# A hybrid stack on one core: the order on TensorE set by another estimate of the engines

## The chip, the cores and the metric

The kernel runs on one core of a Trainium2 chip. The metric is the device time of one execution in microseconds; the time of a kernel is the median of its runs. PE is TensorE, DVE is VectorE, ACT is ScalarE, POOL is GpSimd, SP is SyncE.

## The reference

`reference(...)` takes 256 tokens of width 1024 in fp32 through two blocks. The first block has two layers. Each norms x, multiplies by one wide matrix, and feeds the columns to three branches whose outputs are put side by side, multiplied by `w_out` and added to x; a gated product with a per-layer input follows. The second block adds a layer of compressed, selected and windowed attention ("nsa"), a layer of attention with forgetting, both with attention to a memory of 256 further tokens, and a gated convolutional FFN behind each. In short:

```
for l in range(2):                              # first block
    z = rms_norm(x) @ w_in[l]
    y = concat(rwkv7_branch(z_a), dsa_branch(z_b), dilated_branch(z_c))
    x = x + y @ w_out[l];  x = x + gated(rms_norm(x), p[l])
x = rms_norm(x)                                 # second block
x = x + nsa_mixer(...) @ w_o[0];    x = x + conv_ffn(...)
x = x + forgetting(...) @ w_o[1];   x = x + conv_ffn(...);   out = rms_norm(x)
```

The recurrent branch `rwkv7_branch` is a scan over tokens with a 64x64 state for each of 6 heads.

## The kernel before

All of it is one function, `tile_hybrid_stack`. Weights stream from DRAM in blocks of 128 rows. The products are to be exact to fp32: ACT rounds a block to its high part `whi`, DVE or GpSimd subtracts it from the raw block for the low part `wlo` (rows `wlo<-wraw,whi`), the activations are split likewise (`k` and `k`), and each product is made in three passes, high by high, high by low, low by high. So a dense product in the trace is a group of three rows on `pz`, each of 128x256 or so, and a block of weights of 128x512 costs ACT and one of DVE and GpSimd an operation.

Work is written as generators ("streams") that emit a step at a time. `Flow.run` runs the streams of a stage together and decides which emits next. There are nine stages: mixer of layer 0, its gate, mixer of layer 1, its gate, nsa mixer, FFN, forget mixer, FFN, last norm. In a stage run for instance the dense products (`dense`), the recurrent chain (`rwkv_chain`, with gram products, the turning of k by transposes into `bkt`, levels, chunks and a group norm), the sparse and dilated attention, the norm's factors (`stats`, `norm_norm_stats`) and the loading of weights (`loading`).

Only PE's order is fixed by the emission (`tc.manual_schedule(engines={PE})`). Which stream emits next follows from an estimate of time: `Flow.tensor` reckons each PE instruction, `Flow.note` each one of the other engines with a rate per element (table `RATE`), and `Clock.settle` lets every engine that is free start the first instruction that is ready, as if the engines did not touch each other. The orders on DVE, ACT, GpSimd and SP are made by the compiler's scheduler from the emitted program, and so change with it. Each engine runs its own queue strictly in order.

Names in what follows: in the first block's mixers the head sums are products of a constant with `k` into a tile of 128x2 (L616, in `rwkv_chain`, for `bon`). In the nsa mixer `norm_norm_stats` makes 1/sqrt by three Newton steps on GpSimd (tiles `rs_t` and `rs_y` of 128x1, two of each for each half of the tokens), DVE writes a diagonal matrix from the result (`diag`), and PE multiplies it by ones (`po<-diag,ones`) so that the factors lie along the columns in all rows. `cmp_part` makes the compressed keys' and values' inputs, `cmp_keys`, `cmp_values` and `cmp_attend` go on from there, `mem_prep` prepares the memory. L616 is the product, L621 the transpose and L458 the place from which all other engines' instructions are issued, so rows are told apart by tiles. `out_rows` sets up the loads of `w_o` in the second block and names the events that they wait for; its first group of layer 0 waits for none.

Of the kernel before, what the change touches and what calls it, by code (L numbers as in the profile page):

```python
# [110 lines left out]
class Ev:  # L111
    """A point in the emission that other streams can wait for."""
# [9 lines left out]
class Fork:  # L122
    """A stream to be started that the one that yields it doesn't wait for."""
# [6 lines left out]
# For each run of streams: the time to allow for what may come in between, and that from or to the tensor engine.  # L130
# [6 lines left out]
class At:  # L137
    """The time when some instructions are through, as far as it can be told."""
# [10 lines left out]
class Op:  # L149
    __slots__ = ("lane", "cost", "deps", "start", "end", "ready")  # L150

    def __init__(self, lane, cost, deps, end=math.inf):
        self.lane, self.cost, self.deps, self.end = lane, cost, deps, end


class Clock:
    """Estimates when the engines are through with what has been emitted.

    An instruction's time follows from its size, its dependences from the regions that it reads and writes. An engine
    that is free starts the first of the instructions that are ready. What lies more than PAST before the present  # L160
    is settled for good.
    """

    PAST = 4.0

    def __init__(self):
        self.now, self.dirty, self.pending = 0.0, False, []
        self.free = {name: 0.0 for name in RATE}
        self.free["SP"] = 0.55
        self.used, self.last, self.owner, self.slots = {}, {}, {}, {}  # L170
        self.pool, self.names, self.prior = {}, {}, {}
        self.reach = 0.2
# [11 lines left out]
    def follows(self, pool, old):  # L184
        """Tiles of a pool take the place of those of an earlier one."""
# [17 lines left out]
    def before(self, reads, writes=(), lane=None):  # L203
        """The instructions that one with these operands comes after; engines that read a bank of PSUM take turns."""
# [35 lines left out]
    def put(self, lane, cost, reads, writes, issuer=None):  # L240
# [5 lines left out]
        op = Op(lane, cost, deps)  # L246
# [5 lines left out]
    def settle(self):  # L252
# [3 lines left out]
        free = dict(self.free)  # L256
# [20 lines left out]
        while True:  # L277
            best = None
            for lane, ops in ready.items():
                f = free[lane]  # L280
                for j, (i, op) in enumerate(ops):
                    key = (max(f, op.ready), i)
# [7 lines left out]
            free[lane] = op.end  # L290
            order.append(op)
# [5 lines left out]
        for op in order:  # L297
            if op.start < self.now - self.PAST:
                self.free[op.lane] = op.end
                op.deps = ()  # L300
# [14 lines left out]
class Flow:  # L315
    """Orders the emission of several streams of work by an estimate of the tensor engine's time.
# [2215 lines left out]
```

## Time and profile before

| | |
|---|---|
| runs, median (all) | 1208.56 us (1205.94, 1208.56, 1211.92) |
| profiled execution, span | 1214.1 us |
| PE busy | 1123.1 us, 92% |
| DVE, ACT, POOL busy | 928.3, 727.0, 362.7 us |
| DMA | 168.60 MB, 139 GB/s mean |

The profile is of one execution. It gives busy time for each engine, the clock that PE was granted (1.0 is 2.4 GHz, 0.5 is 1.2 GHz), the chain of work that ended last, and for each wait of an engine what released it. Times of rows are microseconds from the start of the span.

### The profile page before, as it was taken

How to read it: one execution, taken by the hardware profiler on the slowest of the kernel's cores; microseconds unless marked ns; L12 is line 12 of the kernel's file. 1: busy time of each engine (PE TensorE's matmuls, PEld its weight loads, DVE VectorE, ACT ScalarE, POOL GpSimd, SP SyncE). 2: the span in 40 equal slices, each digit the busy share in tenths (PEclk: the TensorE clock that was granted, in tenths of full speed). 3: DMA queues.
4: the chain of work that ended last, by engine and by line, in shares of the span. 5: the costliest groups of instructions: out<-in, count | busy, mean ns of one | idle time of the engine just before them, and what ended most of it. 6: DMA issues, size and time to landing. Idle time of an engine off the chain costs nothing.

```text
span 1214.1 us, 23478 instructions
## 1 busy us (share of the span) xinstructions
PE 1123.1 (92%) x8505; PEld 1000.8 (82%) x8505; DVE 928.3 (76%) x2246; ACT 727.0 (60%) x1642; POOL 362.7 (30%) x355
## 2 busy tenths in 40 slices
PE   6899999988989989979989899999989998999996
PEld 6888887888888867978856899999878867999995
DVE  4889887768898877868777677777777666877786
ACT  4526656656266666666556566666666555766664
POOL 4442213433521226160001612222251124222221
PEclk9879989989899999988979999999989999999999
DMA  7444324444452146647312456666534424666662
GB/s 213 111 125 122 80 53 139 139 140 109 119 141 80 45 134 213 194 116 212 101 35 51 153 152 204 192 187 181 185 92 140 139 84 145 183 191 186 188 183 95
DMA packets 154124, 168.60 MB, mean 139 GB/s; under 512 B 15692, under 2 KB 141532, under 8 KB 154008
## 3 DMA queue, kind: packets, MB, share of 16 engines
q1 hardware_dynamic: 153336, 166.10, 46.9%
q0 software_dynamic: 672, 1.00, 0.4%
q8 instruction: 67, 1.10, 0.4%
q14 instruction: 49, 0.40, 0.1%
HBM read 164.65 MB, written 2.42 MB: 138 GB/s over the span
## 4 chain that ended last, share of the span: by engine, by line
PE 64%; issue 13%; DVE 10%; POOL 8%; ACT 4%; DMA 1%; SPq 0%; ACTq 0%; POOLq 0%; DVEq 0%
PE pz L616 34%; PE po L616 9%; PE pr L616 7%; PE sc L616 7%; POOL k L458 4%; PE tp L616 3%; PE tp L621 3%; POOL wlo L458 2%; DVE k L458 2%; DVE wlo L458 2%; ACT whi L458 2%; POOL rs_t L458 1%; POOL rs_y L458 1%; PE pr L621 1%; DVE zs L458 1%
## 5 line engine op out<-in xcount | busy, mean ns | idle before, releaser
L458 ACT ACTIVATE whi<-wraw 128x512 fp32r<-128x512 f32 (+2 forms) x604 | 371.2, 624 | 248.9 <-PE pz L616 72.5
L458 DVE TENSOR_TENSOR wlo<-wraw,whi 128x512 fp32r<-128x512 f32 (+1 forms) x505 | 365.1, 736 | 141.8 <-ACT whi L458 131.7
L616 PE MATMUL pz<-k,whi 128*128 128x256 f32 x1568 | 314.0, 297 | 7.7 <-ACT k L458 4.9
L616 PEld LDWEIGHTS pz<-k,whi 128*128 128x128 f32 x1568 | 255.8, 200 | 18.5 <-issue 5.8
L458 POOL TENSOR_TENSOR wlo<-wraw,whi 128x512 fp32r<-128x512 f32 (+3 forms) x99 | 132.9, 1344 | 415.9 <-ACT whi L458 378.4
L616 PE MATMUL pz<-whi,k 128*128 128x256 f32 (+5 forms) x1152 | 248.9, 302 | 8.4 <-DVE k L458 5.0
L616 PE MATMUL pz<-k,wlo 128*128 128x256 f32 x784 | 229.1, 292 | 10.2 <-POOL wlo L458 10.2
L616 PEld LDWEIGHTS pz<-whi,k 128*128 128x128 f32 (+1 forms) x1152 | 187.2, 188 | 20.3 <-DVE k L458 6.9
L458 POOL TENSOR_TENSOR k<-yv,k 128x256 fp32r<-128x256 f32 x54 | 95.6, 1785 | 280.8 <-ACT k L458 280.8
L616 PE MATMUL pz<-wlo,k 128*128 128x256 f32 (+5 forms) x576 | 170.6, 296 | 0.1
L616 PEld LDWEIGHTS pz<-k,wlo 128*128 128x128 f32 x784 | 157.2, 200 | 11.5 <-POOL wlo L458 11.5
L616 PE MATMUL po<-k,whi 128*128 128x256 f32 x704 | 132.1, 281 | 0.0
L616 PEld LDWEIGHTS pz<-wlo,k 128*128 128x128 f32 (+1 forms) x576 | 108.5, 188 | 3.3 <-DVE wlo L458 0.6
L616 PEld LDWEIGHTS po<-k,whi 128*128 128x128 f32 x704 | 109.0, 191 | 0.0
L616 PE MATMUL po<-k,wlo 128*128 128x256 f32 x352 | 98.8, 281 | 0.0
L616 PE MATMUL sc<-whi,k 128*128 128x512 f32 x240 | 82.2, 402 | 3.8 <-POOL k L458 3.5
L458 DVE SCALAR_TENSOR_TENSOR k<-zs,convp,k 128x254 f32<-128x254 f32 (+1 forms) x176 | 73.7, 482 | 0.0
L458 ACT ACTIVATE sm<-sm,mn 128x128 f32<-128x128 f32 x100 | 44.4, 445 | 37.9 <-DVE mn L458 37.8
L616 PEld LDWEIGHTS po<-k,wlo 128*128 128x128 f32 x352 | 67.0, 190 | 0.0
L616 PE MATMUL tp<-whi,k 128*128 128x512 f32 x176 | 58.8, 395 | 0.0
L616 PEld LDWEIGHTS sc<-whi,k 128*128 128x128 f32 x240 | 45.1, 189 | 15.9 <-POOL k L458 4.8
L616 PE MATMUL sc<-wlo,k 128*128 128x512 f32 x120 | 47.4, 395 | 0.0
(372 smaller groups left out, 1858.5 us busy)
## 6 DMA issues: line engine op xcount, KB each, us to landing
wraw<-in_w_up_dram SPq DMA_DIRECT2D x88, 512.0 KB
wraw<-in_w_in_dram SPq DMA_DIRECT2D x44, 512.0 KB
wraw<-in_w_down_dram SPq DMA_DIRECT2D x44, 512.0 KB
wraw<-in_w_in_dram SPq DMA_DIRECT2D x32, 256.0 KB
wraw<-in_w_out_dram SPq DMA_DIRECT2D x16, 512.0 KB
wraw<-in_ple_w_gate_dram SPq DMA_DIRECT2D x16, 512.0 KB
wraw<-in_w_o_dram SPq DMA_DIRECT2D x10, 512.0 KB
wraw<-in_w_kv_shared_dram SPq DMA_DIRECT2D x10, 512.0 KB
```

The costliest lines, as they stand in the source:

```text
L458: ins = call(*args, **kw)
L616: nc.tensor.matmul(out_, st, mv, start=start, stop=stop)
L621: nc.tensor.transpose(out_, x, idn)
```

## The change

The estimate of `Flow` and `Clock` is changed in three ways, and one load is held back.

1. Instructions that hold the SBUF port that DVE and GpSimd share are reckoned one after another: every instruction on GpSimd, and on DVE those with more than two elements a row that read more than one larger SBUF operand, or that are a `tensor_scalar` or `tensor_copy` from SBUF to SBUF.
2. `Flow.tensor` reckons 2200 columns a us for fast products of 256 columns or more (2400 before; half of it at the lower clock), and products overlap if they use different row groups or different column groups of the array (16 parts; before 4, by columns alone).
3. The first `w_o` group of the nsa layer is loaded only when all loads of the layer's input weights have begun (`Begun`).

```diff
-        self.quiet, self.issue, self.lanes, self.work = False, 0.0, [0.0] * 4, {}
+        self.quiet, self.issue, self.lanes, self.work = False, 0.0, [0.0] * 16, {}
...
-                    key = (max(f, op.ready), i)
+                    key = (max(f, op.ready, held) if op.port else max(f, op.ready), i)
...
             free[lane] = op.end
+            if op.port:
+                held = op.end
...
-        op = self.clock.put(lane, cost, reads, writes, issuer)
+        port = lane == "POOL"
+        if lane == "DVE" and n > 2:
+            big = [x for x in reads if x.space != PSUM and math.prod(x.shape[1:]) > 1]
+            port = len(big) > 1 or name in ("tensor_scalar", "tensor_copy") and len(big) == 1 and writes[0].space != PSUM
+        op = self.clock.put(lane, cost, reads, writes, issuer, port)
...
-        lanes = range(*(x // 32 for x in (self.clock.region(out)[1], self.clock.region(out)[2] + 31)))
+        r0, r1, c0, c1 = (x // 32 for ap in (st, out) for x in (self.clock.region(ap)[1], self.clock.region(ap)[2] + 31))
+        lanes = [4 * r + c for r in range(r0, r1) for c in range(c0, c1)]
...
+        full = 2200 if mv.dtype != F32 and cycles >= 256 else 2400
...
-            rate = 2400 if self.work.get(k - 1, 0) >= BUSY else 1200
+            rate = full if self.work.get(k - 1, 0) >= BUSY else full / 2
...
+class Begun:
+    def __init__(self, chain):
+        self.chain = chain
+    @property
+    def n(self):
+        return self.chain().left
...
-        u = Load(OP_SHARE, [yT2_ev[l][k] for k in ks] if l or ks != OUT_2[0][0] else ())
+        u = Load(OP_SHARE, [yT2_ev[l][k] for k in ks] if l or ks != OUT_2[0][0] else [Begun(lambda: chains["nsa", 0])])
```

`Chain` counts in `left` the loads that have not begun. No instruction of the program is added or removed on any engine (PE 7649, DVE 2216, ACT 1472, POOL 360, SP 404); about 1090 of PE's change places, 403 in the mixer of layer 0, 424 in that of layer 1, 190 in the nsa mixer, 56 in the forget mixer and under 15 in each other stage. Lines L616, L621 and L458 become L638, L643 and L469.

The first place is on PE in the mixer of layer 0. `pr` with 128x2 are the head sums, `sc` scores of the sparse attention, `pz` dense products with weights `whi` and `wlo`. Before:

```order
L616 MATMUL pz_1148<-whi_0_0_1050,k_1_92 128x256
L616 MATMUL pz_1148<-wlo_0_0_1051,k_1_92 128x256
L616 MATMUL pz_1148<-whi_0_0_1050,k_2_93 128x256
L616 MATMUL pr_1202<-cst_74,k_107_887 128x2 x6
L616 MATMUL sc_1212<-k_6_99,k_132_1114 128x256 x2
L616 MATMUL pz_1148<-whi_2_0_1054,k_1_92 128x256
```

On PE in the same mixer after the change:

```order
L638 MATMUL pz_1368<-whi_4_0_1314,k_3_94 128x256
L638 MATMUL pz_1368<-wlo_4_0_1315,k_3_94 128x256
L638 MATMUL pz_1368<-whi_4_0_1314,k_4_95 128x256
L638 MATMUL pr_1440<-cst_74,k_112_910 128x2 x6
L638 MATMUL pz_1368<-whi_6_0_1324,k_3_94 128x256
L638 MATMUL pz_1368<-wlo_6_0_1325,k_3_94 128x256
```

The head sums stood in the eleventh group of dense products and now stand near the end of the thirteenth; all of the twelfth has moved ahead of them. The mixer of layer 1 shows the same.

The second place is on PE at the start of the nsa mixer. `po<-diag,ones` spreads the norm's factors, `pz<-k,whi` and `pz<-k,wlo` are the products of `cmp_part`, `pz<-whi,mT` those of the memory's values. Before:

```order
L616 MATMUL pz_6955<-k_973_6671,whi_4_0_6947 128x256
L616 MATMUL pz_6955<-k_974_6672,whi_4_0_6947 128x256
L616 MATMUL pz_6955<-k_973_6671,wlo_4_0_6948 128x256
L616 MATMUL po_7032<-diag_6869,ones 128x128
L616 MATMUL po_7032<-diag_6871,ones 128x128
L616 MATMUL pz_6955<-k_973_6671,whi_6_0_6951 128x256
L616 MATMUL pz_6955<-k_974_6672,whi_6_0_6951 128x256
```

On PE at the start of the nsa mixer after the change:

```order
L638 MATMUL pz_6884<-wlo_6_0_6867,mT_6113 128x256
L638 MATMUL pz_6884<-whi_6_0_6866,mT_6114 128x256
L638 MATMUL po_6942<-diag_6852,ones 128x128
L638 MATMUL po_6942<-diag_6854,ones 128x128
L638 MATMUL pz_6884<-whi_6_0_6866,mT_6113 128x256
L638 MATMUL pz_6884<-wlo_6_0_6867,mT_6113 128x256
L638 MATMUL pz_6884<-whi_6_0_6866,mT_6114 128x256
L638 MATMUL pz_6960<-k_971_6669,whi_0_0_6901 128x256
```

The two products have moved from the last sixth of the compression's 48 products to the place ahead of all of them.

The third place is on GpSimd at the same time: its four splits of the compression's weights and the Newton steps. Before:

```order
L458 TENSOR_SCALAR rs_t_6745<-rs_y_6744,ss_6741 128x1
L458 TENSOR_SCALAR rs_t_6754<-rs_y_6753,ss_6739 128x1
L458 TENSOR_SCALAR rs_y_6744<-rs_t_6745,rs_y_6744 128x1
L458 TENSOR_TENSOR wlo_0_0_6902<-wraw_6897,whi_0_0_6901 128x512
L458 TENSOR_SCALAR rs_y_6753<-rs_t_6754,rs_y_6753 128x1
L458 TENSOR_TENSOR wlo_2_0_6906<-wraw_6897,whi_2_0_6905 128x512
```

On GpSimd there after the change:

```order
L469 TENSOR_TENSOR wlo_0_0_6902<-wraw_6897,whi_0_0_6901 128x512
L469 TENSOR_TENSOR wlo_2_0_6906<-wraw_6897,whi_2_0_6905 128x512
L469 TENSOR_SCALAR rs_t_6745<-rs_y_6744,ss_6741 128x1
L469 TENSOR_SCALAR rs_t_6754<-rs_y_6753,ss_6739 128x1
L469 TENSOR_TENSOR wlo_4_0_6953<-wraw_6899,whi_4_0_6952 128x512
L469 TENSOR_SCALAR rs_y_6744<-rs_t_6745,rs_y_6744 128x1
```

Two splits now come ahead of the first Newton step; the second pair of splits lies between the first steps, as before it did a little later.

## Rows read from the trace of the kernel before

**Rows 1.** The page, part 4: the chain that ended last.

```profile
PE 64%; issue 13%; DVE 10%; POOL 8%; ACT 4%; DMA 1%; SPq 0%; ACTq 0%; POOLq 0%; DVEq 0%
```

**Rows 2.** Busy time by stage: window, us, engines' busy (instructions), PEclk, DMA share, GB/s.

```profile
0.00:226.70 226.70, 201.99 (x1662) 177.63 (x1663) 173.60 (x461) 121.21 (x295) 79.75 (x81) 0.94 0.43 117
...
262.00:471.00 209.00, 191.69 (x1644) 168.73 (x1645) 168.17 (x454) 114.67 (x283) 72.03 (x70) 0.94 0.40 111
...
508.00:677.50 169.50, 154.00 (x1061) 125.67 (x1062) 129.25 (x413) 107.87 (x293) 32.98 (x48) 0.91 0.39 110
```

**Rows 3.** Waits of PE by cause: us in total, times, longest.

```profile
PE pz L616 <- POOL wlo L458: 10.2, 6, 3.5
```

**Rows 4.** Timeline of DVE and POOL, 521 to 527 us: start, us, instruction.

```profile
521.96 0.69 DVE L458 TENSOR_TENSOR wlo<-wraw,whi 128x512 fp32r<-128x512 f32 x1 [0.93 <-ACT whi L458]
523.21 2.99 DVE L458 TENSOR_TENSOR wlo<-wraw,whi 128x512 fp32r<-128x512 f32 x1 [0.55 <-ACT whi L458]
...
523.15 2.49 POOL L458 TENSOR_TENSOR wlo<-wraw,whi 128x512 fp32r<-128x512 f32 x2
```

**Rows 5.** Stretches at half clock, columns as in rows 2.

```profile
321.30:328.10 6.80, 6.80 (x30) 6.13 (x30) 6.17 (x10) 1.39 (x2) 3.61 (x2) 0.50 0.29 43
...
532.90:539.70 6.80, 5.02 (x23) 5.02 (x24) 2.13 (x3) 4.44 (x11) 2.70 (x8) 0.50 0.28 76
...
614.80:628.50 13.70, 12.11 (x52) 7.09 (x52) 8.30 (x40) 8.86 (x33) 0.00 (x0) 0.50 0.09 24
```

**Rows 6.** Timeline of PE in both first-block mixers, idle before and releaser in brackets.

```profile
103.71 1.40 PE L616 MATMUL pr<-cst,k 128*128 128x2 f32 x12
...
110.41 0.58 PE L621 MATMUL pr<-cst,bk 64*128 64x64 f32 x6 [1.39 <-ACT bkt L458]
...
176.44 0.63 PE L621 MATMUL tp<-cst,qr 128*128 128x128 f32 x4 [2.22 <-ACT sm L458]
...
201.11 0.49 PE L616 MATMUL pr<-wlo,k 128*128 128x512 f32 x1 [1.30 <-DVE wlo L458]
...
319.41 0.79 PE L616 MATMUL pr<-k,bk 64*128 64x128 f32 x5 [2.19 <-DVE k L458]
...
357.63 0.58 PE L621 MATMUL pr<-cst,bk 64*128 64x64 f32 x6 [1.96 <-ACT bkt L458]
...
426.14 0.63 PE L621 MATMUL tp<-cst,qr 128*128 128x128 f32 x4 [1.22 <-DVE qr L458]
```

**Rows 7.** Timeline of PE at the start of the nsa mixer.

```profile
521.26 0.40 PE L616 MATMUL pz<-k,whi 128*128 128x256 f32 x2
...
524.46 0.39 PE L616 MATMUL pz<-k,wlo 128*128 128x256 f32 x1 [1.36 <-POOL wlo L458]
...
526.16 0.28 PE L616 MATMUL pz<-k,wlo 128*128 128x256 f32 x1
...
528.64 0.29 PE L616 MATMUL pz<-k,wlo 128*128 128x256 f32 x1
...
534.68 0.80 PE L616 MATMUL po<-diag,ones 128*128 128x128 f32 x2 [5.53 <-DVE diag L458]
...
536.56 0.41 PE L616 MATMUL pz<-whi,k 128*128 128x256 f32 x1
```

**Rows 8.** Timeline of POOL there: Newton steps, two in a row.

```profile
526.61 0.66 POOL L458 TENSOR_SCALAR rs_t<-rs_y,ss 128x1 f32<-128x1 f32 x2
...
528.33 1.72 POOL L458 TENSOR_SCALAR rs_t<-rs_y,ss 128x1 f32<-128x1 f32 x2
...
533.53 0.55 POOL L458 TENSOR_SCALAR rs_y<-rs_t,rs_y 128x1 f32<-128x1 f32 x2
```

**Rows 9.** Timeline of PE in the middle and at the end of the nsa mixer.

```profile
562.36 0.28 PE L616 MATMUL pz<-whi,k 128*30 128x256 f32 x1
...
570.44 0.41 PE L621 MATMUL pz<-cst,k 30*128 30x30 f32 x2 [1.88 <-DVE k L458]
...
606.84 1.06 PE L616 MATMUL pz<-kcT,k 128*128 128x32 f32 x8
...
616.35 2.03 PE L621 MATMUL tp<-cst,k 128*128 128x128 f32 x7 [3.62 <-DVE ls L458]
```

More of the change, by code (lines that the diff above doesn't have):

```diff
@@ L149, with __init__ @@
 class Op:
-    __slots__ = ("lane", "cost", "deps", "start", "end", "ready")
-    def __init__(self, lane, cost, deps, end=math.inf):
-        self.lane, self.cost, self.deps, self.end = lane, cost, deps, end
+    __slots__ = ("lane", "cost", "deps", "start", "end", "ready", "port")
+    def __init__(self, lane, cost, deps, end=math.inf, port=False):
+        self.lane, self.cost, self.deps, self.end, self.port = lane, cost, deps, end, port
 class Clock:
@@ L169, in __init__ @@
         self.free["SP"] = 0.55
+        self.port = 0.0
         self.used, self.last, self.owner, self.slots = {}, {}, {}, {}
@@ L238, in when, with put @@
         return max((o.end + self.gap(o.lane, lane) for o in ops), default=0.0)
-    def put(self, lane, cost, reads, writes, issuer=None):
+    def put(self, lane, cost, reads, writes, issuer=None, port=False):
         deps = self.before(reads, writes, lane)
@@ L245, in put @@
             deps = [first]
-        op = Op(lane, cost, deps)
+        op = Op(lane, cost, deps, port=port)
         self.mark(op, reads, writes)
@@ L255, in settle @@
         self.dirty = False
-        free = dict(self.free)
+        free, held = dict(self.free), self.port
         wait = {}
@@ L299, in settle @@
                 self.free[op.lane] = op.end
+                if op.port:
+                    self.port = op.end
                 op.deps = ()
@@ L756, in __init__ @@
         def __init__(self, loads):
-            self.loads, self.ahead, self.then, self.last = iter(loads), None, None, None
+            loads = list(loads)
+            self.loads, self.ahead, self.then, self.last, self.left = iter(loads), None, None, None, len(loads)
         def begin(self):
@@ L762, in begin @@
                 if self.ahead is not None:
+                    self.left -= 1
                     self.ahead.prev, self.last = self.last, self.ahead
```

## The prediction

> **What bounds the kernel now.** I read the page first: the chain that ended last runs over PE for 64% of the span and over waits for other engines for most of the rest [rows 1]. So the time is PE's work plus the places where PE stands still, plus what PE loses by running at the lower of its two clock levels. The table by stage says where that is: PE is idle 24.7 us of the first layer's mixer (226.7 − 202.0), 17.3 us of the second layer's (209.0 − 191.7) and 15.5 us of the mixer that opens the second block (169.5 − 154.0); these three stages also have the low mean clocks, 0.94, 0.94 and 0.91 [rows 2]. Everywhere else PE is nearly full. The order of instructions hardly moves outside these three stages, so the whole answer must come from some 57 us of idle time and the stretches at half clock inside them.
>
> The list of PE's waits names POOL's splitting of weights as the costliest single cause (10.2 us in 6 waits) [rows 3]. One row shows why: VectorE's split of a 128x512 block took 0.69 us while GpSimd was quiet and 2.99 us when GpSimd ran two such splits (2.49 us) over the same stretch [rows 4]. VectorE and GpSimd thus hold up each other, and the planner of before knows nothing of it. The planner's rate for dense products is off too: from the row at 526.16 to that at 528.64, at full clock, PE starts 21 products of 256 columns in 2.48 us, 0.118 us each, some 2170 columns a us where the planner reckons 2400 [rows 7]. The new figures are nearer the trace. That does not settle the time, since the planner only chooses the order on PE, and the orders of the other engines then shift with it.
>
> **The change part by part.** No instruction is added or removed; PE has the same work. The terms are waits that go, waits that come, and clock.
>
> *First layer's mixer.* The head sums of the recurrent branch (the row with 128x2 outputs at 103.71) move behind all of one group of dense products and most of the next. 48 products and some 60 of the next pass them, about 110 × 0.118 = 13 us. The chain that follows (turning k, the levels, the group norm) starts some 13 us later and is left with less other work under it at the end, and the gating work of the other branches comes earlier. Four waits stood behind the old place. The one for the turned k was 1.39 us [rows 6]; ACT's copies stood there behind the scalings of a projection and one weight split, and now directly follow, so I take 0.4 (−1.0). The one for a scaled tile before the transposes at 176.44 was 2.22 us [rows 6]; the gates it waits for now come more than 10 us earlier in all queues: −2.2. The one for w_out's low half at 201.11 was 1.30 [rows 6]; VectorE has less queued there: −1.0. Against it, attention transposes that had cover now lie 3 to 5 us behind what they read. By the nearest rows such a wait costs 0.4 to 2.2 us, and I count two, +2.0. Sum −2.2, ends −4.2 (no new wait) and +0.2 (both at the top).
>
> *Second layer's mixer.* The same move of the head sums, with the same shape of order. The wait for the turned k, 1.96 us, becomes 0.6 (−1.4); the one at 426.14, 1.22, goes (−1.2) [rows 6]; the split of w_out repeats that of the first layer (the row at 201.11 stands for both): −1.0; two new waits of one us less in all than above: +1.5. Here 9 dense products also move ahead of the gram products at 319.41, which waited 2.19 us for VectorE [rows 6]. 9 × 0.118 = 1.0 us of cover: −1.0. The 6.80 us after that wait ran at half clock [rows 5]. If PE stays full through it, 3.4 us come back; I count half, −1.7. Sum −4.8, ends −8 and 0.
>
> *Clock in the two level phases.* The dense work that now runs ahead of the head sums used to fill the stretch of small products behind them. By the orders some 33 dense products lay between the small ones there before, and 12 now. The trace shows no case of that very mix. The nearest row is the tail of the nsa mixer, small products only, where the clock stood at 0.50 for 13.70 us; the other end is no loss, since the first layer's phase ran at full clock before. A stretch of 3.4 us at half clock in one and 0 to 3.4 in the other costs 1.7 to 3.4: I take +2, ends 0 and +7 (13.7 / 2) [rows 5].
>
> *Entry of the nsa mixer.* Here the change costs. The two products that spread the norm's factors over all rows (out of `diag`) stood behind the compression's products and PE reached them late; it still waited 5.53 us for the second one, after 1.36 us for GpSimd's split at 524.46 [rows 7]. They now stand ahead of the compression's 48 products. PE gets there at 521.26 − 3 × 0.118 = 520.9 and stops until the Newton steps on GpSimd are through. How early can that be? The chain's steps are small: two of one kind took 0.66 and two of the other 0.55 when undisturbed, but a pair took 1.72 beside VectorE [rows 8]. The last twelve ran from 528.33 to 534.08, 5.75 us, and undisturbed would take 3 × (0.66 + 0.55) = 3.6. The new orders put VectorE's `diag` writes directly behind one split, so VectorE will mostly wait too and not disturb; I take the spread at 531.5 instead of 534.68, with 534.7 (nothing gained) and 530.6 as ends. From there PE has 2 + 3 + 48 products and, later, the 8 transposes (0.8 us) to catch up. After a stop of 5.53 us the next 6.80 us ran at 0.50 [rows 5, 7], with 0.21 us a product. So 0.4 + 32 products in 6.8 us + 19 × 0.118 = 2.2, and 0.8: PE is even at 541.7. Before it was there at 536.56 with 3.1 us of half clock still ahead, which cost 1.6: 538.1 [rows 5, 7]. Loss 541.7 − 538.1 = +3.6; ends 0 and +7. Behind the waiting spread stand ACT's scalings of x and the splits of the next weights; they have 10 us of idle ahead of PE's need, so nothing more is charged.
>
> After a stop about twice as long the same 6.80 us at half clock are assumed. The Trainium skill, in "TensorE: Matmul & The Clock Gate", section "HAM oscillation", has the same view: each wait that is long enough makes the burst behind it start cold, once, and its price is half of the throttled time. By that the longer stop would cost no more clock than the shorter, as the sum has it; the stretch from 532.90 at 0.50 agrees.
>
> *Middle of the nsa mixer.* The wait for the compressed keys, 1.88 us, stays. From the last of the keys' products (562.36) to their transposes (570.44) lie 8.0 us of work on other engines [rows 9]. For the compressed values PE has 2.9 us of work in that interval where it had 10.3: by the keys' latency a wait of up to 5 us, by the steps' earlier places in VectorE's queue none. I take half, +2.5, ends 0 and +5.
>
> *End of the nsa mixer.* Attention scores and memory transposes move behind the dense products, so that 6.6 us of PE work instead of 4.3 stand between the compressed scores (ending at 607.9) and the transposes that waited until 616.35, 8.5 us later. That wait, 3.62 us and 0.5 more before it, falls to 8.5 − 6.6 = 1.9 [rows 9]: −2.2. Half clock over 13.7 us behind it [rows 5] may shorten a little: −0.3 in the sum, up to −3.5 at the end. Sum −2.5, ends −6 and +1.
>
> The later w_o load has the same place in SyncE's queue, and the forget mixer has a few swaps of neighbours without a long wait beside them: 0, with ±1. PLE gates and both FFNs keep their order: 0.
>
> Sum: −2.2 − 4.8 + 2.0 + 3.6 + 2.5 − 2.5 = −1.4 us. On the profiled execution's 1214.1 that is 1212.7; the profiled execution lies 5.5 us over the median of 1208.56, so 1207.2 in the measure of the runs.
>
> **The rivals.**
>
> *Dense work spent too early (slower).* Place: entry and middle of the nsa mixer and the two level phases. The planner believes PE finds enough between; if the spread is ready only at 534.7, the values wait the full 5 us and one level phase falls to half clock for as long as the tail did, the terms are +7, +5 and +7, against gains of −1, −3 and −2.5: +12.5, some 1221. It decides from about 533.5 on for the spread, with a wait over 3 us at the values. For it: PE does stand for 10 us with 48 products ready behind the spread [rows 7]. Against: GpSimd's queue has nothing else then [rows 8].
>
> *Waits go as planned and the clock stays up (faster).* Gram, tail and level phases keep the full level, no new waits: −4.2 − 8 + 0 + 0 + 0 − 6 = −18; half of that already passes 0.5%. About −12 is its middle: 1196. For it: the costliest cause of PE's waits comes from the contention that the planner now counts [rows 3, 4]. Against: a stall at the nsa entry is in the order itself.
>
> *The change doesn't do what it says.* The planner could still be off by as much as before, since the true durations of GpSimd vary from 0.28 to over 1 us a step [rows 8]: the waits change places and the sum is 0 ± 3, 1208. This lies within the forecast's own band.
>
> **How the numbers follow.** About 0.5%, 6 us, can be told from no change. Forecast (with the third rival inside it): 1207, within 6 us of the median, 0.42. Faster: 0.33. Slower: 0.25. The likeliest case's own range is 1202.5 to 1214.6. The range for 8 in 10 goes to the faster case's middle less some, 1193, and to the slower one's, 1220.
>
> **What would show it.** In the changed profile: PE's wait for `diag` at the nsa entry near 10 us instead of 5.5, and GpSimd's 24 steps closer together; idle before the turned k under 1 us in both layers; no wait at the scaled transposes; w_out's wait under 0.5 us; a wait of 1 to 5 us at the compressed values; idle time at the end of the nsa mixer down to 2 us. Mean clocks: first layer 0.93 to 0.95, second 0.94 to 0.96, nsa 0.89 to 0.92. The forecast is wrong if the level phases lose the clock for long, if the spread comes at 528 or at 536, or if stages whose order hardly moves change by over 2 us.

## The result and the profile after

The changed kernel takes 1269.3 us (median of its runs, 1261.8 to 1269.4) against 1209.2 us of the kernel before on the same chip: a ratio of 1.047, 95% interval 1.044 to 1.050. It is **slower by 4.7%**, and far above the forecast of 1207 and its range of 1193 to 1220. The profiled execution has a span of 1267.6 us, 53.5 more than that of before (1214.1).

The chain that ended last, from the page of the changed kernel (it answers to [rows 1]):

```profile
PE 36%; issue 10%; POOL 5%; DVE 4%; ACT 2%; DMA 1%; SPq 0%; POOLq 0%; ACTq 0%; DVEq 0%
```

This line says little here: only 58% of the span is accounted for, so its falling share of PE is not a finding. The table by stage does better. These are the same three stages of the changed kernel as in [rows 2], with the same columns:

```profile
0.00:241.40 241.40, 207.72 (x1661) 183.47 (x1662) 172.77 (x461) 122.28 (x295) 77.18 (x82) 0.92 0.40 110
276.70:506.60 229.90, 199.91 (x1644) 175.20 (x1645) 171.42 (x454) 114.91 (x283) 73.56 (x70) 0.90 0.36 101
544.20:730.40 186.20, 158.06 (x1061) 127.06 (x1062) 125.78 (x413) 108.48 (x293) 29.23 (x48) 0.88 0.35 100
```

The three stages are 14.7, 20.9 and 16.7 us longer, 52.3 together: practically all of it. The window minus PE's busy time is 33.7, 30.0 and 28.1 us where it was 24.7, 17.3 and 15.5, so PE stands still for 34.3 us more. The other 18.0 us are busy time of PE: the same products take longer. The granted clock fell from 0.94, 0.94 and 0.91 to 0.92, 0.90 and 0.88. With two levels, 1.2 and 2.4 GHz, twice the missing part is the share of time at the lower one: some 38.6, 46.0 and 44.7 us against 27.2, 25.1 and 30.5, by clocks of two digits. PE loses half of such time where it has work, which is at most 23 us in the three and fits the 18.0, since PE also idles at the lower level.

The list of PE's waits by cause, of the changed kernel (us in total, times, longest), has a new head; [rows 3] showed GpSimd's splits there:

```profile
PE po L638 <- DVE diag L469: 11.9, 3, 6.7
PE pr L638 <- DVE s L469: 11.8, 2, 7.3
PE tp L643 <- ACT k L469: 10.7, 3, 5.3
...
PE tp L643 <- DVE kd L469: 5.4, 1, 5.4
...
PE pz L638 <- POOL wlo L469: 3.9, 5, 1.7
```

The wait that the change was aimed at did fall, from 10.2 us to 3.9. The four other rows come to 39.8 us; of these causes the first had 9.1 us before, the second 0.9. The timeline of PE in the two first-block mixers, which answers to [rows 6]:

```profile
88.80 0.61 PE L638 MATMUL pz<-whi,k 128*128 128x296 f32 x1 [2.96 <-DVE zs L469]
...
119.66 0.90 PE L643 MATMUL tp<-cst,qr 128*128 128x128 f32 x3 [3.59 <-ACT k L469]
...
126.31 1.40 PE L638 MATMUL pr<-cst,k 128*128 128x2 f32 x12
...
138.60 1.67 PE L638 MATMUL pr<-k,k 64*64 64x64 f32 x26 [2.59 <-DMA k<-bounce_t]
...
160.07 0.91 PE L638 MATMUL pr<-s,k 64*64 64x64 f32 x12 [4.53 <-DVE s L469]
...
378.29 0.90 PE L643 MATMUL tp<-cst,qr 128*128 128x128 f32 x3 [5.25 <-ACT k L469]
384.12 1.39 PE L638 MATMUL pr<-cst,k 128*128 128x2 f32 x12
...
417.70 0.91 PE L638 MATMUL pr<-s,k 64*64 64x64 f32 x12 [7.29 <-DVE s L469]
```

The head sums (outputs of 128x2) stand at 126.31 in the first layer, where before they stood at 103.71. In both kernels the tile that they read is there at about 88 us. They wait for more, because their stream waits for all that it has emitted, and that includes the small triangular solve on VectorE. Its first and last step in the changed kernel, from VectorE's timeline:

```profile
92.15 0.17 DVE L469 TENSOR_TENSOR r<-r,r 96x15 f32<-96x15 f32 x1
...
108.21 1.27 DVE L469 TENSOR_TENSOR r<-r,r 96x15 f32<-96x15 f32 x1
```

That is 17.3 us. The same steps of the kernel before, from VectorE's timeline:

```profile
92.76 0.39 DVE L458 TENSOR_TENSOR r<-r,r 96x15 f32<-96x15 f32 x2
...
106.69 0.17 DVE L458 TENSOR_TENSOR r<-r,r 96x15 f32<-96x15 f32 x1
```

They took 14.1 us. The planner's own estimate of them in this layer was 8.5 us with the old model and is 20.4 with the new one: 5.6 us too low became 3.1 us too high. The new estimate is the nearer one, and with it the sums and everything behind them went far back.

What that meets on the other engines is seen at the two worst places. Before 417.70, first the product on PE that the copy of the chunk's state reads, then VectorE's timeline:

```profile
408.24 0.57 PE L638 MATMUL pr<-uv,k 128*64 128x64 f32 x12
```

```profile
405.53 0.43 DVE L469 MAX8 m<-k 128x8 f32<-128x256 f32 x1
...
416.06 0.41 DVE L469 MATCH_REPLACE8 k<-m,k 128x256 f32<-128x256 f32 x1
...
417.29 0.36 DVE L469 COPY s<-pr 128x192 f32<-128x192 f32 x1
```

The copy of the chunk's state (417.29), for which PE waits, is queued on VectorE behind the whole search for the largest scores, 11 us long, although the product that it reads was through at 408.81. On VectorE in the kernel before:

```profile
380.00 0.36 DVE L458 COPY s<-pr 128x192 f32<-128x192 f32 x1
...
383.03 0.42 DVE L458 MAX8 m<-k 128x8 f32<-128x256 f32 x1
```

There the first of these copies ran ahead of that search, the next two lay between its steps, and the last came behind it. VectorE did not take the copy of 417.29 ahead of its turn, though the product was there. The Trainium skill, in "TensorE: Matmul & The Clock Gate", section "Architectural detail: the array is 16× 32×32, not 1× 128×128", states that VectorE's queue is strictly first in, first out, and these rows agree. Before 378.29, from the timelines of SyncE's queue and of ACT:

```profile
352.11 9.68 SPq L469 DMA_DIRECT2D wraw<-in_w_in_dram  x4
...
367.65 1.75 SPq L469 DMA_DIRECT2D bounce_t<-r  x4
369.50 4.31 SPq L469 DMA_DIRECT2D wraw<-in_w_in_dram  x3
```

```profile
374.48 1.15 ACT L469 ACTIVATE whi<-wraw 128x512 fp32r<-128x512 f32 x2 [3.99 <-DMA wraw<-in_w_in_dram]
```

SyncE issues four weight loads, until 361.79, then stands until the solve's result can be stored (`bounce_t<-r`, 367.65), and only then issues the next weights. ACT then stands 3.99 us on the weights with the copy for PE behind it in its queue. In the kernel before six weight loads were issued ahead of that store:

```profile
334.37 14.40 SPq L458 DMA_DIRECT2D wraw<-in_w_in_dram  x6
353.02 1.76 SPq L458 DMA_DIRECT2D bounce_t<-r  x4
```

In the first sparse mixer, PE (answering to [rows 7, 9]), then GpSimd [rows 8]:

```profile
544.31 0.66 PE L643 MATMUL sc<-cst,x 128*128 128x128 f32 x4 [1.16 <-ACT gth L469]
...
563.91 0.76 PE L638 MATMUL po<-diag,ones 128*128 128x128 f32 x2 [6.67 <-DVE diag L469]
567.80 0.80 PE L638 MATMUL po<-diag,ones 128*128 128x128 f32 x2 [3.12 <-DVE diag L469]
...
618.05 0.31 PE L643 MATMUL tp<-cst,kd 30*128 30x30 f32 x1 [5.42 <-DVE kd L469]
```

```profile
556.78 1.08 POOL L469 TENSOR_SCALAR rs_t<-rs_y,ss 128x1 f32<-128x1 f32 x2
...
566.65 0.55 POOL L469 TENSOR_SCALAR rs_y<-rs_t,rs_y 128x1 f32<-128x1 f32 x2
```

PE stands 6.67 and 3.12 us before the norm's factors, until the last Newton step ends at 567.2. It stands 5.42 us more for the compressed keys, a chain of short steps on VectorE:

```profile
611.11 0.20 DVE L469 TENSOR_TENSOR kd<-pz,cb 30x64 f32<-30x64 f32 x1
...
612.93 0.69 DVE L469 TENSOR_TENSOR wlo<-wraw,whi 128x512 fp32r<-128x512 f32 x1 [1.40 <-ACT whi L469]
...
617.83 0.16 DVE L469 COPY kd<-kd 30x64 f32<-30x64 f32 x1
```

Six steps of 0.16 to 0.21 us are spread over 6.9 us, because splits of weights and steps of the attention lie between them.

### The profile page after: what moved, and what is told of

Its sections match the earlier page's. It is cut to its first block, busy times and chain, and to the rows that moved or that the text cites. A ratio compares the mean times of both kernels' runs of the same rounds, so it can differ in the third digit from the quotient of the medians.

```text
span 1267.6 us, 23484 instructions
## 1 busy us (share of the span) xinstructions
PE 1139.6 (90%) x8505; PEld 1011.8 (80%) x8505; DVE 928.0 (73%) x2246; ACT 729.3 (58%) x1642; POOL 358.5 (28%) x355
## 4 chain that ended last, share of the span: by engine, by line
PE 36%; issue 10%; POOL 5%; DVE 4%; ACT 2%; DMA 1%; SPq 0%; POOLq 0%; ACTq 0%; DVEq 0%
PE pz L638 17%; PE po L638 8%; PE sc L638 6%; POOL k L469 3%; PE tp L638 3%; PE tp L643 1%; POOL wlo L469 1%; DVE k L469 1%; POOL rs_t L469 1%; DVE sm L469 1%; ACT whi L469 1%; ACT k L469 1%; DVE wlo L469 1%; ACT sm L469 1%; POOL rs_y L469 0%
## 5 line engine op out<-in xcount | busy, mean ns | idle before, releaser
L469 ACT ACTIVATE whi<-wraw 128x512 fp32r<-128x512 f32 (+2 forms) x604 | 370.4, 624 | 263.1 <-PE pz L638 83.6
L469 DVE TENSOR_TENSOR wlo<-wraw,whi 128x512 fp32r<-128x512 f32 (+1 forms) x505 | 362.0, 731 | 157.7 <-ACT whi L469 147.2
L638 PE MATMUL pz<-k,whi 128*128 128x256 f32 x1568 | 309.3, 294 | 6.8 <-ACT k L469 4.8
L638 PEld LDWEIGHTS pz<-k,whi 128*128 128x128 f32 x1568 | 254.1, 199 | 17.3 <-issue 6.7
L638 PE MATMUL pz<-whi,k 128*128 128x256 f32 (+5 forms) x1152 | 256.9, 308 | 10.6 <-DVE k L469 5.1
L469 POOL TENSOR_TENSOR wlo<-wraw,whi 128x512 fp32r<-128x512 f32 (+3 forms) x99 | 134.3, 1359 | 448.8 <-ACT whi L469 378.7
L638 PE MATMUL pz<-k,wlo 128*128 128x256 f32 x784 | 227.5, 290 | 5.7 <-POOL wlo L469 3.7
L638 PEld LDWEIGHTS pz<-whi,k 128*128 128x128 f32 (+1 forms) x1152 | 192.4, 193 | 21.6 <-DVE k L469 6.9
L469 POOL TENSOR_TENSOR k<-yv,k 128x256 fp32r<-128x256 f32 x54 | 97.2, 1814 | 283.4 <-ACT k L469 283.4
L638 PE MATMUL pz<-wlo,k 128*128 128x256 f32 (+5 forms) x576 | 172.8, 300 | 1.0 <-DVE wlo L469 0.7
L638 PEld LDWEIGHTS pz<-k,wlo 128*128 128x128 f32 x784 | 155.7, 199 | 7.1 <-POOL wlo L469 4.6
L638 PE MATMUL po<-k,whi 128*128 128x256 f32 x704 | 131.6, 280 | 0.0
L638 PEld LDWEIGHTS pz<-wlo,k 128*128 128x128 f32 (+1 forms) x576 | 111.3, 193 | 4.0 <-DVE wlo L469 1.6
L638 PEld LDWEIGHTS po<-k,whi 128*128 128x128 f32 x704 | 108.3, 190 | 0.0
L638 PE MATMUL po<-k,wlo 128*128 128x256 f32 x352 | 98.6, 280 | 0.0
L638 PE MATMUL sc<-whi,k 128*128 128x512 f32 x240 | 81.2, 399 | 3.8 <-POOL k L469 3.5
L469 DVE SCALAR_TENSOR_TENSOR k<-zs,convp,k 128x254 f32<-128x254 f32 (+1 forms) x176 | 73.4, 476 | 0.0
L638 PEld LDWEIGHTS po<-k,wlo 128*128 128x128 f32 x352 | 66.7, 190 | 0.0
L469 ACT ACTIVATE sm<-sm,mn 128x128 f32<-128x128 f32 x100 | 44.4, 445 | 33.9 <-DVE mn L469 33.7
L638 PE MATMUL tp<-whi,k 128*128 128x512 f32 x176 | 58.5, 393 | 0.0
L638 PEld LDWEIGHTS sc<-whi,k 128*128 128x128 f32 x240 | 44.8, 188 | 16.0 <-POOL k L469 4.8
L638 PE MATMUL sc<-wlo,k 128*128 128x512 f32 x120 | 47.2, 393 | 0.0
```

What stands on the lines that cost most here:

```text
L469: ins = call(*args, **kw)
L638: nc.tensor.matmul(out_, st, mv, start=start, stop=stop)
```

## The experiments

Every run is given with its ratio to the kernel before on the same chip. "Stage 0", "2" and "4" are the first layer's mixer, the second layer's mixer and the first sparse mixer; their lengths go from PE's first instruction of a stage to its first of the next, in the profiled execution (221.5, 212.4 and 169.4 us before; +15.3, +20.8 and +16.7 after). These columns are of that one execution, which in `late_sums` took 8 us more than the median and in `bounce_on_pool` and `before_bounce` 6.5 to 7 us less. Numbered or lettered theories in the expectations are explained in them; the question of each group stands ahead of it.

| run | median us | ratio, 95% interval | stage 0, 2, 4 |
|---|---|---|---|
| the change | 1269.3 | 1.047 (1.044 to 1.050) | +15.3, +20.8, +16.7 |
| port_alone | 1241.8 | 1.025 (1.022 to 1.029) | +6.0, +8.6, +18.1 |
| rate_alone | 1236.8 | 1.021 (1.019 to 1.024) | +1.0, +7.2, +12.5 |
| lanes_alone | 1230.7 | 1.016 (1.014 to 1.018) | −1.0, +3.7, +7.5 |
| late_sums | 1215.8 | 1.004 (1.002 to 1.006) | +5.2, +3.0, +0.8 |
| tiny | 1231.2 | 1.016 (1.013 to 1.019) | −2.6, +11.0, +8.4 |
| tiny_down | 1221.0 | 1.009 (1.006 to 1.013) | −1.1, −0.7, +7.0 |
| after_tiny | 1256.3 | 1.036 (1.031 to 1.040) | +14.2, +10.0, +11.0 |
| bounce_on_pool | 1256.2 | 1.037 (1.033 to 1.041) | +12.2, +9.2, +11.5 |
| narrow_topk | 1253.9 | 1.034 (1.031 to 1.037) | +15.3, +12.4, +16.2 |
| before_bounce | 1230.1 | 1.014 (1.010 to 1.018) | +2.3, +9.4, −3.6 |
| sums_on_need | 1244.5 | 1.027 (1.024 to 1.030) | +9.6, +2.7, +14.8 |
| need_and_bounce | 1240.9 | 1.024 (1.021 to 1.027) | +7.8, +2.8, +13.9 |
| before_need | 1236.5 | 1.021 (1.018 to 1.025) | +10.7, +9.0, +3.7 |
| after_late_spread | 1259.0 | 1.042 (1.038 to 1.045) | +8.9, +21.0, +11.8 |
| need_and_late_spread | 1239.7 | 1.028 (1.023 to 1.034) | +6.6, +8.5, +7.7 |

**Which of the three terms does it?** Each term was put into the kernel before alone (the guard that goes with the rate is an order of starting that moves nothing by itself).

```
port_alone:   the port's rule;  full = 2400;  lanes by column groups
rate_alone:   no port;          full = 2200;  lanes by column groups
lanes_alone:  no port;          full = 2400;  lanes = 4 r + c
```

> Only the serialising of instructions that share the port is kept in the estimate; rate, row groups and the held-back load are as before. Theory 1 (the port term alone makes the loss, because it lets the planner believe that the recurrent chain of each first-block mixer and the Newton steps of the nsa mixer end much later or earlier than other work): 1255 to 1275, the first-block mixers 12 to 25 us longer each. Rival (the loss needs the three terms together, or comes from rate and row groups): under 1225.

> Only the rate of 2200 columns a us in the estimate, with the held-back load, without which the planner's streams block each other at this rate. Theory 1: 1195 to 1220, head sums at their old place. Rival (the order of before is a tuned optimum and any other estimate loses tens of us): 1230 or more.

> Only the 16 row and column groups in the estimate. Theory 1: 1195 to 1220. Rival (any change of the order loses): 1230 or more.

All three cost, 1.6 to 2.5%, and added up they would cost 6.2% where the whole costs 4.7. So no single term is at fault. The port's 1241.8 lies between the two forecasts for it, the other two came out as their rivals said. In `rate_alone` and `lanes_alone` the head sums stand within 20 of PE's places of where they stood before, and the loss is there all the same. Nor is it seen that the terms cost by what they model: the port term, which alone takes account of the contention in [rows 4], lengthens stage 4 most of all.

**Are the late head sums enough?** The kernel before, with nothing but a longer wait in front of the sums, so that they stand on PE within two instructions of where they stand after the change:

```
-        yield WAIT
+        yield flow.mine(11.0)
```

> The kernel before with one edit: the stream of the recurrent branch waits 11 us longer (by the old estimate) before its second head sums, in both layers. They then stand on PE within two instructions of the place that they have in the changed kernel. Theory 2 (the late head sums alone make the loss of the two first-block mixers): 1235 to 1250, these two mixers 12 to 20 us longer each and all other stages within 2 us of before. Rival (the loss comes from the rest of the new order on DVE and SP): under 1220.

It costs 0.4%. The theory that the place of the sums alone makes the loss in the first-block mixers fell.

**Does any other order cost as much?** The planner's fixed cost of a VectorE instruction is 0.069 us. One nanosecond more or less says nothing about the chip and moves some 415 of PE's instructions.

```
-RATE = {"DVE": (0.069, 1 / 960), ...
+RATE = {"DVE": (0.070, 1 / 960), ...     tiny (in before), after_tiny (in after)
+RATE = {"DVE": (0.068, 1 / 960), ...     tiny_down (in before)
```

> A control: the kernel before, where the estimate's fixed cost of a VectorE instruction is 0.070 us instead of 0.069. That is no statement about the chip, and still over 400 of PE's instructions change places. Theory 3 (the order of before is a good draw out of many: its waits and lags were chosen for just these estimates, so nearly any other estimate gives a longer time): 1218 to 1240. Rival (the loss of the changed kernel and of its three parts comes from what these model): 1204 to 1214.

> The kernel before with VectorE's fixed cost in the estimate at 0.068 us instead of 0.069; nothing else, and 415 instructions of PE stand elsewhere. Theory A (the order before is the good one of many, and any other estimate loses it): 1225 to 1245 us, ratio 1.013 to 1.03, as with 0.070 (1231 us). Theory B (0.070 was unlucky, and a change of one nanosecond is worth nothing on average): 1200 to 1216 us, ratio 0.993 to 1.006.

> The kernel after with VectorE's fixed cost in the estimate at 0.070 us instead of 0.069; 427 instructions of PE stand elsewhere than in the kernel after. Theory A (the new estimate is no worse than the old one, but orders of both lie anywhere from 1.2 to 5 per cent above the kernel before): it differs from 1269 us by 10 us or more, to either side, and lies anywhere from 1225 to 1280. Theory C (what costs is in the three terms: the head sums behind the whole solve, the weight loads behind the stores of the solve, the lanes' dense spread): these stand where they stood, so 1260 to 1278 us, ratio 1.043 to 1.057.

A nanosecond upwards costs 1.6%, as much as a whole term of the change; a nanosecond downwards costs 0.9%, less than the 1.3% that I had set as the lower end; a nanosecond in the changed kernel gains 13 us. So some 10 to 20 us come and go with the draw of the order, for no reason that the estimate could name, and the order before is a good draw. Where such time goes shows in the second layer's mixer of `tiny`, in the columns of [rows 2]:

```profile
258.80:479.00 220.20, 200.34 (x1645) 175.67 (x1646) 171.73 (x454) 115.40 (x283) 73.56 (x70) 0.91 0.39 106
```

It is 11.2 us longer than the 209.0 of before, but PE idles only 2.6 us more (19.9 against 17.3). The rest is PE's busy time, the same work at a mean clock of 0.91 instead of 0.94. That the waits' new places bring the lower level with them is not shown by this one profile: an execution's own share can be some 6 us of it (below).

**Do the queues hold the work up as the trace says?** In the changed kernel, with PE's order unchanged (VectorE's shifts a little): the solve's stores and loads issued from GpSimd's queue, so that no weight load stands behind them; or the search on 32 columns (which leaves out most of the search). And the first of these in the kernel before.

```
-            Y.dma_start(bview(bounce_t, b), tb[24 * b:24 * b + 24])
+            Timed(flow, nc.gpsimd, "SP").dma_start(bview(bounce_t, b), tb[24 * b:24 * b + 24])
...
-                V.max(m8, acc)
+                nc.vector.max(m8, acc[:, 0:32])
```

> The changed kernel with the same order on PE; the recurrent branch's stores of the solved blocks to DRAM and their loads back are issued from GpSimd's queue instead of SyncE's, 6 a layer. Theory 4 (in the changed kernel weight loads stand behind these stores in SyncE's queue, which waits there for VectorE's solve, and ScalarE's and then PE's waits at the scaled transposes, 3.6 and 5.3 us, come from that): 1250 to 1260, both waits under 1 us. Rival (the loads come late for lack of slots): 1264 to 1274.

> The changed kernel with the same order on PE; the eight top-k rounds of the sparse attention work on 32 columns instead of 128 or 256, which leaves out most of the search. Theory 5 (VectorE, which runs its queue in order, has the search of the second tile ahead of the first chunk's state, and PE's waits of 4.5 and 7.3 us for that state are the price): 1248 to 1258, both waits under 1.5 us. Rival (the state is late anyway): 1262 to 1274.

> The kernel before, its order on PE unchanged, with the solve's stores and loads by way of DRAM issued from GpSimd's queue instead of SyncE's. In the kernel before SyncE has most weight loads ahead of these stores (six at 334 to 349 us, the store at 353), so there is little to free: ratio 0.995 to 1.003 if the theory of the held queue explains only the kernel after; 0.985 to 0.993 if the stores hold weight loads in the kernel before as well; above 1.005 if GpSimd, which pays for each issue and also splits the weights, is the worse place.

The first two give 13 and 15 us back, within the forecast times, but the waits did less than was expected. In `narrow_topk` the two waits for the state copy fall from 4.53 and 7.29 to 3.42 and 2.41 us: the way the queue says, and not to the 1.5 expected. In `bounce_on_pool` the store no longer holds any load, and yet PE's waits at the transposes are still there: 4.34 us in the first layer (3.59 after the change) and 4.79 in the second. The second layer's rows on PE, ACT and VectorE:

```profile
375.92 0.90 PE L643 MATMUL tp<-cst,qr 128*128 128x128 f32 x3 [4.79 <-ACT k L469]
```

```profile
374.04 0.42 ACT L469 ACTIVATE gth<-zs 128x256 f32<-128x256 f32 x1 [4.63 <-DVE zs L469]
```

```profile
372.00 0.29 DVE L469 MAX8 m<-k 128x8 f32<-128x128 f32 x1
...
373.32 0.68 DVE L469 TENSOR_TENSOR zs<-pz,wide 128x512 f32<-128x512 f32 x1
```

ACT no longer stands on the weights but on the next thing, a scaled tile that VectorE makes in the middle of the search. In the changed kernel that tile was through at 374.56, just after the weights had let ACT go on (374.48): the weights were one of two causes that came at nearly the same time. What taking one away gave, 0.46 us at this place, can't be told from nothing, since in `after_late_spread`, where nothing stands elsewhere up to there, the same wait is 3.95 us.

What did go in `bounce_on_pool` is the longest wait of all, the 7.29 us for the state copy in the second layer. The edit also shifts VectorE's order, and there the copy stands behind two of the search's eight rounds and no longer behind all:

```profile
407.38 0.42 DVE L469 MAX8 m<-k 128x8 f32<-128x256 f32 x1
...
408.35 0.36 DVE L469 COPY s<-pr 128x192 f32<-128x192 f32 x1
```

So this run's 13 us are no measure of what SyncE's queue cost; they speak as much for the search. In the kernel before, the same edit costs 1.4%, which is the case "GpSimd is the worse place"; VectorE's order shifts there too, so that the place alone is not shown to cost it. There the stage that loses (stage 2, +9.4) has some 3 us more idle time and 10 us more at half clock.

**Is it the wait for too much in front of the sums?** The sums wait for their own tile alone; then with the bounces moved as well; then in the kernel before.

```
-        yield WAIT
+        yield from flow.need(rk)
```

> The changed kernel with one edit: the stream of the recurrent branch waits before its second head sums only for the tile that they read, and no longer for the solve and the stores beside it. The head sums then come some 250 places earlier on PE than in the changed kernel and 130 earlier than before. Theory 2 in its weaker form (late head sums push the whole chain to where nothing covers it): 1235 to 1250, the first-block mixers 10 to 18 us shorter each than in the changed kernel. Rival (the head sums matter little, by the run that only moved them): 1258 to 1275.

> The kernel after with two edits at once: the head sums wait for their own tile alone (alone 1244.5 us, 25 less than after), and the solve's stores and loads by way of DRAM are issued from GpSimd's queue instead of SyncE's (alone 1256 us, 13 less). If the two undo different waits (head sums too late on PE in one place, SyncE's weight loads held behind stores in the other), the gains add: 1228 to 1238 us, ratio 1.016 to 1.024. If they undo the same waits (head sums early let the stores leave early, so that the weight loads aren't held), the second adds little: 1241 to 1248 us, ratio 1.026 to 1.032.

> The kernel before with the head sums waiting for their own tile alone, as in sums_on_need; 666 instructions of PE stand elsewhere. Theory A (the order before is the good one of many): 1215 to 1240 us, ratio 1.005 to 1.025, although the sums' wait is told more truly. If the sums' place is worth time by itself, as the 25 us in the kernel after say: 1195 to 1206 us, ratio 0.988 to 0.997.

In the changed kernel this gives 25 us back, the most of any single edit; stage 2 loses 2.7 us instead of 20.8, stage 0 still 9.6. The 7.29 us for the state copy are 1.82 here. Moving the bounces too adds 4 us, which the intervals don't tell from nothing, and not 13, so the two undo largely the same waits. But in the kernel before the same truer wait costs 2.1%, 28 us. The early place of the sums is thus worth 25 us in the one order and minus 28 in another: it has no price of its own.

**Does the first sparse mixer lose what its two longest waits show?** Two longer waits for this stage alone; on PE only four instructions change place.

```
-        yield flow.mine(SPREAD_LAG)
+        yield flow.mine(SPREAD_LAG + (6.0 if flow.nth == 4 else 0.0))
...
             G.memset(kc_, 0.0)
-            yield WAIT
+            yield flow.mine(5.0)
```

> The kernel after with two longer waits in the first sparse mixer's planner: the spread of the norm's scales 6 us later, the transposition of the compressed keys 5 us later. On PE only 4 instructions change place against the kernel after (the spread stands some 50 instructions further on). Theory D (that stage is longer because these two stand too early for VectorE, by 9.8 and 5.4 us of waiting, and the dense work behind them could have run): the two waits fall under 5 us together, the stage shortens by 8 to 15 us, 1254 to 1262 us. Theory E (the work moved ahead of the waits is only lent, and what needs VectorE's scales waits later): the stage changes by under 4 us, 1265 to 1273 us.

> The kernel after with the head sums waiting for their own tile alone (alone 1244.5 us) and the two longer waits in the first sparse mixer. Theory D: the gains add, since they lie in different stages: 1229 to 1238 us, ratio 1.015 to 1.022. Theory E: 1241 to 1248 us.

The waits move rather than go. PE's rows of `after_late_spread`:

```profile
558.75 0.38 PE L638 MATMUL po<-diag,ones 128*128 128x128 f32 x2
...
564.33 0.80 PE L638 MATMUL po<-diag,ones 128*128 128x128 f32 x2 [5.20 <-DVE diag L469]
...
610.20 0.42 PE L643 MATMUL pz<-cst,k 30*128 30x30 f32 x2 [6.21 <-DVE k L469]
```

The first half of the spread costs nothing now, but the second still waits 5.20 us, and the 5.42 us for the keys have become 6.21 us for the values, which stood next. The stage is 4.9 us shorter: less than the 8 to 15 of the one theory, more than the under 4 of the other. How little of that can be read, the windows of stages 0 and 4 of this run say:

```profile
0.00:235.40 235.40, 202.51 (x1665) 178.12 (x1666) 173.81 (x461) 122.06 (x295) 79.54 (x82) 0.94 0.40 113
...
536.80:717.00 180.20, 153.76 (x1053) 123.85 (x1053) 125.12 (x410) 107.28 (x291) 30.74 (x47) 0.91 0.37 103
```

Stage 0, in which nothing stands elsewhere, took 235.4 us where the profile after has 241.4, with an idle time that differs by 0.8 us and a clock of 0.94 for 0.92. Stage 2 of `sums_on_need` and of `need_and_late_spread`, again one order, differ by 5.8 us in the table. A single profile thus places a stage to within some 6 us, and differences below that in the table should not be read; the 4.9 us are among them, so neither theory is decided by the stage. The median falls by 10 us, the ratio by 0.6%, with intervals that still touch. Together with `sums_on_need` the two longer waits give 1239.7 us, and the intervals of the two overlap: no gain that can be told.

## Why the prediction was wrong, point by point

**What bounds the kernel** was read rightly: PE's stops and its clock in three stages. 52.3 of the 53.5 us lie in them. One reading beside it was wrong: at the split of 0.69 us (521.96) GpSimd was not quiet: it ended a split at 522.07 and made two small Newton steps from there, 1.11 us long where such a pair else takes 0.66. That two GpSimd splits lengthen one on VectorE to 2.99 us stands.

**The waits that were to go** mostly went. The turned k waits 0.32 us instead of 1.39 (predicted 0.4), in the second layer no longer at all; the transposes of 176.44 and 426.14 no longer wait (those of 119.66 and 378.29 after the change are earlier ones of the same tile's name); the gram products wait 0.93 instead of 2.19; the splits by GpSimd 3.9 instead of 10.2 in all. The second layer's w_out was missed: 2.95 us where 1.0 was to be saved of 1.29. But for that the gains were about as forecast.

**The waits that come** is the step that failed first. I counted two in the first layer for 2.0 us and less in the second, "by the nearest rows" of 0.4 to 2.2 us. The first layer has 2.96 (88.80), 3.59 (119.66), 2.59 (138.60), 4.53 (160.07) and 2.6 (206 to 210): 16.3 us. The second has 1.82, 5.25 and 7.29 and a few smaller. Idle time went up by 9.0 and 12.7 us where −2.2 and −4.8 stood for waits and half a stretch of clock. The nearest rows were waits of an order that put no such block behind a whole search. Their size says nothing about what happens when a block that PE needs ends up behind 11 us of search, or weight loads behind a store that waits for a solve. I had asked how many dense products pass the head sums, not what stands on the three other queues between the sums' readers and PE. The move itself was right as a count (116 of PE's places in the first layer) and undersized in time: 13 us forecast, 22.6 measured, with the stops of 2.96 and 3.59 us on the way.

**The clock** was the second: +2 us with an end at +7. By the granted clock of the first two stages the share at the lower level rose by 11.4 and 20.9 us, worth up to 16. The mean clocks of 0.93 to 0.95 and 0.94 to 0.96 became 0.92 and 0.90. The level phases were the wrong place to look; each of the new long stops has a stretch at half clock that begins within it or as it ends, and I had none of these stops. Such stretches of the changed kernel, for the stops that end at 160.07, 417.70 and 567.80, with the columns of [rows 5]:

```profile
159.90:163.30 3.40, 3.23 (x23) 3.11 (x24) 2.50 (x9) 1.73 (x6) 0.00 (x0) 0.50 0.02 5
412.50:422.70 10.20, 5.00 (x32) 4.88 (x33) 6.13 (x21) 3.35 (x10) 0.84 (x1) 0.50 0.00 0
559.20:572.90 13.70, 5.87 (x26) 5.60 (x27) 2.22 (x4) 4.41 (x8) 9.52 (x26) 0.50 0.24 69
```

The last of them is twice the 6.80 us that the sum assumed at the entry of the sparse mixer, but PE had only 5.87 us of work in it.

**The entry of the sparse mixer** was right in mechanism and size. The factors are spread at 567.80, which on the clock of before (both start this stage with the same instruction, 36.18 us apart) is 531.62; 531.5 was forecast, and a wait near 10 us (9.8). Some 340 instructions into the stage PE is 3.3 us later than before (559.45 before, 598.93 after, less the 36.18); a loss of 3.6 was forecast.

**Its middle and end** were not. The wait for keys and values grew by 4.8 us (1.22 and 5.42 instead of 1.88), the upper end of that term, at the keys and not at the values. At the end 3.46 us still stand before the transposes, and 1.98 and some 3 us of attention waits have come. By the same count PE is 8.4 us late after 640 instructions and 16.7 at the last of the 1061: the end costs some 8 us, where −2.5 was forecast.

**The rivals.** "Dense work spent too early" had the right sign and the right place in part (chance 0.25), and a price of 12.5 us that was about a fifth of the 60. The largest mistake is one of the frame, not of a term: the sum treated the order as a base from which named moves add and subtract. The runs show that the order before is better than every neighbour that was tried. Two orders from a nanosecond in a constant, without any reason to be worse, cost some 10 and 20 us, and none of the thirteen other kernels came down to the time before (`late_sums`, at 0.4%, came nearest). A forecast for a reordering of so many instructions had to begin at plus 1 to 2%, not at zero.

**What stays open.** Of the 60 us, some 25 go with the sums' wait for too much, but that edit redraws the order as well, and a nanosecond alone gave 13 of the 60 back; some 10 to 20 are what a redraw cost in the two that were tried, and how the rest divides is not settled. With the sums mended, alone or with the bounces or the spread, the kernel stays at 1240 to 1245 us, about where each single term (1231 to 1242) and `before_need` (1237) lie, and no edit of it came nearer. Whether the planner's other constants would suit the new one after being set anew was not tried.

## What to carry to other kernels

Where a planner sets the order by estimates, first change a constant by an amount that means nothing: what that costs is the least that any change of the model has to beat, and an order that is already good can have mostly losses around it, as here. A truer estimate of one cost is not by itself a better order, as long as the planner's other waits (here one for all that a stream has emitted) ask for more than they need. When a block moves on PE, read the queues of the other engines at its new place, SyncE's too, and when a wait has been traced to its last releaser, ask which other one would have come a moment earlier. When an edit moves work from one queue to another, read the orders of all engines again before the gain is put down to the queue.

## What the runs showed of the hardware

The same order of the same stage ran with a mean clock of 0.92 in one profile and 0.94 in another, 6 us apart, with idle times within 0.8 us. So of a difference between two single profiles the clock can be the larger part: in `tiny` 2.6 us of added idle time went with 11.2 us of added length, not all of which need belong to the order. GpSimd's queue took 2.87 us to issue the four stores (in `before_bounce`, at 356.21) that SyncE's issued in 1.76 (the kernel before, at 353.02).
